# Attention's end in a hybrid decoder block: fillers that end 7 steps sooner, and the first out-projection row tile made piece by piece beside the last head's scores

## The chip, the cores and the metric

The kernel runs on one core of a Trainium2 chip. The metric is the device time of one execution in microseconds (us). The core's engines are TensorE (PE in the profile, with its weight loads as PEld), VectorE (DVE), ScalarE (ACT), GpSimd (POOL) and SyncE (SP), which here issues nearly all DMAs.

## The reference, cut to what matters

One block on 2048 tokens of width 1024, in float32: a norm with shift and scale from a condition vector, one input projection to q, k, v (512 each, 8 heads of 64) and u (512), stick-breaking attention on q, k, v, a pooling mixer on u, one output projection of both, a gated residual with a norm, and then the same frame around a SwiGLU feed-forward part.

```python
h = rmsnorm(x, g_mix_pre) * (1.0 + scale_m) + shift_m
q, k, v, u = jnp.split(h @ w_in, [SB_WIDTH, 2 * SB_WIDTH, 3 * SB_WIDTH], axis=-1)
# attention, strictly causal: for a query t and keys s < t
#   logw[t, s] = logsigmoid(z[t, s]) + sum over s < j < t of logsigmoid(-z[t, j])
attn = stick_breaking_attention(q, k, v)
pool = pooling_mixer(u, w_pool, pool_scale)
mix = jnp.concatenate([attn, pool], axis=-1) @ w_out
x = x + gate_m * rmsnorm(mix, g_mix_post)
h = rmsnorm(x, g_ffn_pre) * (1.0 + scale_f) + shift_f
f = (silu(h @ w_gate) * (h @ w_up)) @ w_down
x = x + gate_f * rmsnorm(f, g_ffn_post)
```

## The kernel before, in words

Matrix products are made from high and low parts. `split` (L56 to L59) casts a float32 tile to its high part on ACT and subtracts that on DVE to get the low part; `mm3` (L64 to L70) makes one product from three matmuls: high by high (L68), low by high (L69), high by low (L70). Three such matmuls of 128x128 by 128x512 are called a piece here.

The program has a prologue (norm, condition, first projections, v), attention from 322 us on, the output projection, and the feed-forward part from about 1040 us to the end.

Attention runs 320 steps: 8 heads, and in each head ten units of a query block of 512 and a key block of 512 or its left neighbours, in the order (0,0); (1,1), (1,0); (2,2), (2,1), (2,0); (3,3) to (3,0); four steps of 128 queries in each. A step of number n issues, in this order: the values product of a step turned three before (`values_step`, two matmuls, L875 and L876); the scores of step n (L827, L828), two sigmoids of them on ACT (L830, L832); one step later the scan that makes the running product on DVE (L843), and the product of both, the weights, on POOL (L849); then the turn of step n − 7 (`turn_step`): four PE transposes (L860) into a PSUM bank of the cycle `t_ps`, split into high (`wth`, ACT) and low (`wtl`, DVE) parts. Steps on the diagonal block are narrower for the scores (128 to 512 wide).

Into the steps go the fillers: the pieces of the remaining projections and small operations of the pooling mixer on POOL. How many pieces are due by a step is `goal`, which grows with the area of the steps so far and reaches its full count after END units of the 80; for END = 78 the last filler matmuls are at step 292, and the small operations end about ten steps behind. The output projection's weights are loaded when the fillers are through (two halves, `hb` and `ha`; one pair of loads in a step).

The output projection has 16 row tiles of 128 tokens, T0 to T15, in the order of SEQUENCE: 0, 4, 1, 5, 2, 6, 3, 7, 8 and so on. For one tile, `mix_load` (L931) loads the mixed rows (attention's and pooling's) and a low part, `mix_add` (L945) adds them on POOL, `mix_split` makes the two halves' high and low parts (`mh`, `ml`), and `mix_products` makes 16 pieces (two column halves by eight row blocks) into two PSUM banks from the cycle `f_ps`. `after_mix` (L1063 to L1084) squares both banks on ACT, makes the reciprocal root with a power on POOL (L113), scales on DVE (L1076), adds the residual on POOL (L1077), and makes the second norm in the same way: a square on ACT (L1080), a power on POOL, a scaling on DVE (L1083). `put_h2` (L1088) transposes the normed rows on PE (L122, `f_pt`) and writes the feed-forward's input.

T0 and T4 are the two first tiles. They are loaded, added and split inside the attention steps, at the step numbers in FIRST_LOADS, FIRST_ADDS and FIRST_SPLITS; their pieces are issued behind the last scores, three in each of the remaining steps (values and turns still come there), and the rest at the end. T1's rows go into memory of a pool (`op0`) that takes the place of attention's; the load waits for one of the last values matmuls.

Three things set the order of the work here. Until `order.close()` each engine gets its instructions in the order in which the code above issues them; behind it, a scheduler sets the order. Each engine runs its own instructions strictly in its order. [...]

Of the kernel before, what the change touches and what calls it, by code (L numbers as in the profile page):

```python
# [43 lines left out]
def block_kernel(ctx, tc, x, c, w_cond, b_cond, g_mix_pre, g_mix_post, w_in, w_pool,  # L44
# [98 lines left out]
    def psum(tag, bufs, name):  # L143
        return psp.tile([P, TB], F32, tag=tag, bufs=bufs, name=name)
# [7 lines left out]
    def bank_cycle(*tags):  # L152
        tags = itertools.cycle(tags)
        return lambda name: psum(next(tags), 1, name) if name else next(tags)

    z_ps, t_ps, av_ps, mm_only = bank_cycle("z0", "z1", "z2"), bank_cycle("w0", "w1"), bank_cycle("a0", "a1"), bank_cycle("mm")
# [661 lines left out]
    def weights_step(u, i):  # L818

        h, tb, sc = u  # L820
        diag = sc == tb
        kt, qt = kv[h, sc][0], qts[h, tb]
        L = (i + 1) * P if diag else TB
        nm = f"{h}_{tb}_{sc}_{i}"
        z = z_ps(f"z{nm}")
        keys = kt[:, 0:L]
        nc.tensor.matmul(z[:, 0:L], qt[:, 0, i * P:(i + 1) * P], keys, start=True, stop=False)  # L827
        nc.tensor.matmul(z[:, 0:L], qt[:, 1, i * P:(i + 1) * P], keys, start=False, stop=True)  # L828
        sg = att.tile([P, TB], F32, tag="sg", bufs=5, name=f"sg{nm}")
        nc.scalar.activation(sg[:, 0:L], z[:, 0:L], AF.Sigmoid, scale=0.125)  # L830
        pr = att.tile([P, TB + 1], F32, tag="pr", bufs=PRB, name=f"pr{nm}")
        nc.scalar.activation(pr[:, 0:L], z[:, 0:L], AF.Sigmoid, scale=-0.125)  # L832
        scans.append((u, i, pr, sg, L, nm))

    def scan_step(u, i, pr, sg, L, nm):

        diag = u[1] == u[2]
        carry = carries.pop(i, None)
        if carry is None:
            nc.gpsimd.memset(pr[:, L:L + 1], 0.0)  # L840
        else:
            nc.gpsimd.tensor_copy(pr[:, L:L + 1], carry)
        nc.vector.tensor_tensor_scan(pr[:, 0:L][:, ::-1], pr[:, 0:L][:, ::-1], begin[:, TB - L:][:, ::-1],  # L843
                                     zero if carry is None else carry, ALU.mult, ALU.max if diag else ALU.bypass)
        if u[2]:
            carries[i] = att.tile([P, 1], F32, tag=f"carry{i}", bufs=2, name=f"carry{nm}")
            nc.gpsimd.tensor_copy(carries[i], pr[:, 0:1])
        w = att.tile([P, TB], F32, tag="w", bufs=OFF + 4, name=f"w{nm}")
        nc.gpsimd.tensor_tensor(w[:, 0:L], sg[:, 0:L], pr[:, 1:L + 1], ALU.mult)  # L849
        wss.setdefault(u, []).append(w)  # L850

    def turn_step(u, b):

        h, tb, sc = u
        i0 = b if sc == tb else 0
        lo0 = i0 * P
        nm = f"{h}_{tb}_{sc}_{b}"
        wt = t_ps(f"wt{nm}")
        for i in range(i0, 4):
            nc.tensor.transpose(wt[:, i * P:(i + 1) * P], wss[u][i][:, b * P:(b + 1) * P], ident)  # L860
        wh = att.tile([P, TB], F32R, tag="wth", bufs=4, name=f"wth{nm}")
        wl = att.tile([P, TB], F32R, tag="wtl", bufs=4, name=f"wtl{nm}")
        split(wh[:, lo0:], wl[:, lo0:], wt[:, lo0:])
        return wh, wl, lo0

    def values_step(u, b, wh, wl, lo0):
        h, tb, sc = u
        hp, j = h // 2, h % 2
        first = sc == tb and b == 0
        last = sc == 0 and b == 3  # L870
        if first:
            avs[h, tb] = av_ps(f"av{h}_{tb}")
        av = avs[h, tb]
        vb = kv[h, sc][1][:, b, :]
        nc.tensor.matmul(av[:, lo0:], vb, wh[:, lo0:], start=first, stop=False)  # L875
        nc.tensor.matmul(av[:, lo0:], vb, wl[:, lo0:], start=False, stop=last)  # L876
        if last:
            end = (h, tb) == (HEADS - 1, NTB - 1)
            o1 = (up if end else wsp).tile([P, TB], F32, tag="um" if end else "o1", bufs=1, name=f"o1_{h}_{tb}")
            nc.scalar.copy(o1, av)  # L880
            for part, dst in enumerate((mtd, mld)):
                (nc.scalar if end else nc.sync).dma_start(dst[tb][hp, j * DH:(j + 1) * DH, :], o1[part * DH:(part + 1) * DH])

    def unit_loads(u):
        h, tb, sc = u
        if sc == tb:
            qts[h, tb] = block_loads(h, tb)
# [17 lines left out]
    area = [2.5 if tb == sc else 4.0 for _, tb, sc in units]  # L905
    wo, wo_next = [], 0
    HB_FREE = N_PIECES - 10 - 18 + 1
    END = 78
    START = 34
    for _ in range(START):  # L910
        next(fill)
# [5 lines left out]
    z_ps, t_ps, av_ps, mm_only = bank_cycle(*('z0', 'z1')), bank_cycle(*('w0', 'w1', 'a1')), bank_cycle(*('a0',)), bank_cycle(*('mm',))  # L917
    steps = [(u, i) for u in units for i in range(4)]

    def wo_load():  # L920
        nonlocal wo_next
        for l in range(2):
            nc.sync.dma_start(raw(wo[wo_next][l]), wod[wo_next][l])
        wo_next += 1
# [1 line left out]

    SEQUENCE = [sb * NT // 2 + half * 4 + i for sb in range(2) for i in range(4) for half in range(2)]
    mixed = {}
    f_ps = bank_cycle("z0", "z1", "z2", "mm", "w0", "w1", "a0", "a1")

    def mix_load(T):  # L931
        tb, cols = T // 4, slice((T % 4) * P, (T % 4 + 1) * P)
        m32 = (wst if T in SEQUENCE[:2] else op0).tile([P, KC, P], F32, tag="w32", name=f"m32_{T}")
        nc.sync.dma_start(m32, mtd[tb][:, :, cols].rearrange("k p t -> p k t"))
        if T in SEQUENCE[:2]:
            if not l32s:
                both = wst.tile([P, 2, TB], F32R, tag="e", bufs=1, name="l32s")
                l32s.extend(raw(both[:, n]).rearrange("p (k t) -> p k t", k=HK) for n in range(2))
            l32 = l32s.pop(0)
        else:  # L940
            l32 = wsp.tile([P, HK, P], F32, tag="o1", bufs=1, name=f"l32_{T}")
        nc.sync.dma_start(l32, mld[tb][:, :, cols].rearrange("k p t -> p k t"))
        return T, m32, l32

    def mix_add(T, m32, l32):  # L945
        nc.gpsimd.tensor_tensor(m32[:, 0:HK], m32[:, 0:HK], l32, ALU.add)
        return T, m32
# [17 lines left out]
                yield  # L965
        mixed[T] = pss

    FIRST_LOADS = (len(steps) - 14, len(steps) - 10)
    FIRST_SPLITS = (len(steps) - 3, len(steps) + 2)
    FIRST_ADDS = (len(steps) - 6, len(steps) - 1)  # L970
    PER_STEP = 3
    firsts, products, l32s = [], [], []

    def mix_pieces(count):
        while products and count:
            if next(products[0], 0) == 0:
                products.pop(0)
            else:
                count -= 1
# [3 lines left out]
    for n in range(len(steps) + OFF):  # L983
        begun = None
        if len(waiting) > LAG:
            begun = waiting.pop(0)
            if begun[1] or begun[0][1] != begun[0][2]:
                values_step(*begun)
                begun = None
        if n < len(steps):  # L990
            u, i = steps[n]
            if i == 0:
                unit_loads(u)
            weights_step(u, i)
            spent += 2.5 if u[1] == u[2] else 4.0
        if len(scans) > 1 or n >= len(steps) and scans:
            scan_step(*scans.pop(0))
        if n >= OFF:
            u, b = steps[n - OFF]
            waiting.append((u, b, *turn_step(u, b)))  # L1000
        if begun is not None:
            values_step(*begun)
        goal = START + (N_PIECES - START) * spent / (4 * sum(area[:END]))
        while fill is not None and taken < goal:
            taken += 1
            if next(fill, 0) == 0:
                fill = None
        for pool, here in ((hb, not wo and taken >= HB_FREE), (ha, len(wo) == 4 and fill is None)):
            if here:
                hi, lo = (pool.tile([P, 4, D], F32R, tag=tag, name=f"wo_{pool.name}{tag}")  # L1010
                          for tag in ("hi", "lo"))
                wo.extend((hi[:, k, :], lo[:, k, :]) for k in range(4))
        if wo_next < len(wo):
            wo_load()
        if n in FIRST_LOADS:
            firsts.append(mix_load(SEQUENCE[FIRST_LOADS.index(n)]))
        if n in FIRST_SPLITS:
            products.append(mix_products(*mix_split(*firsts.pop(0))))
        if n in FIRST_ADDS:
            firsts[0] = mix_add(*firsts[0])  # L1020
        if n >= len(steps):
            mix_pieces(PER_STEP)
    for a in waiting:
        values_step(*a)
        mix_pieces(PER_STEP)
# [90 lines left out]
    steps = []  # L1116
# [406 lines left out]
    steps, ops1_at = halves()  # L1523
# [91 lines left out]
```

## Time and profile before

| what | value |
|---|---|
| time, median of 3 runs | 2313.9 us (2313.23 to 2316.85) |
| the profiled execution's own time | 2318.17 us |
| its span | 2316.4 us (1.77 us lie outside it) |
| its mean granted PE clock | 0.993 of full speed |
| PE busy | 2261.0 us (98% of the span) |
| DVE busy | 1619.1 us (70%) |
| POOL busy | 1311.2 us (57%) |
| ACT busy | 1163.7 us (50%) |
| chain that ended last | PE 81%, DVE 7%, POOL 2%, DMA 2% |

The profile is of one execution, 4.3 us above the median of the runs. Busy times overlap, and a recorded matmul is longer than the time until the next one starts, so a PE that is 98% busy still has room. The view of stretches gives for each stretch its length, the busy time (and the number of instructions) of PE, PEld, DVE, ACT and POOL, then the granted PE clock, the DMA engines' share and GB/s. In timelines the columns are the start, the time it took, the engine, line, operation, output and inputs, the tile's shape, and how many alike follow one another; in brackets stands how long the engine was idle before, and what ended that.

### The profile page before, as it was taken

What the parts mean: (1) busy time and instruction counts of PE and PEld (TensorE: products, weight loads), DVE (VectorE), ACT (ScalarE), POOL (GpSimd) and SP (SyncE); (2) the same over time, 40 slices, a digit from 0 to 9 for tenths busy, and PEclk for the clock granted to TensorE, in tenths of its full rate; (3) what the DMA queues carried; (4) which work ended last, traced back from release to release, by engine and by line L of the source; (5) the groups of instructions that cost most, each with busy time, mean ns of one, the idle gap of its engine ahead of it and who ended that gap; (6) DMA issues with size and microseconds to landing.
All of it is one profiled execution on the core that took longest, in us unless ns stands there. A gap on an engine that the chain in (4) does not pass through costs nothing.

```text
span 2316.4 us, 33051 instructions
## 1 busy us (share of the span) xinstructions
PE 2261.0 (98%) x10605; PEld 1848.3 (80%) x10605; DVE 1619.1 (70%) x2215; ACT 1163.7 (50%) x2414; POOL 1311.2 (57%) x1616
## 2 busy tenths in 40 slices
PE   8999999999999999999999999999999999999997
PEld 4777878888888778887888888788888888888885
DVE  6764559999999966657656565887766556565556
ACT  4433659989998854444323222554433323234444
POOL 4452347787878845555787777331476565641004
PEclk9999999999999999999999999999999999999998
DMA  8885764433435535664545555876854333328554
GB/s 299 269 277 190 288 182 115 120 95 108 125 106 160 168 123 193 209 216 159 164 160 166 159 166 170 285 240 205 262 162 132 95 114 91 114 93 287 188 196 145
DMA packets 307114, 405.14 MB, mean 175 GB/s; under 512 B 19254, under 2 KB 179578, under 8 KB 303868
## 3 DMA queue, kind: packets, MB, share of 16 engines
q1 hardware_dynamic: 302620, 400.68, 54.0%
q10 hardware_dynamic: 4320, 2.36, 0.4%
q8 instruction: 83, 1.36, 0.2%
q14 instruction: 91, 0.75, 0.1%
HBM read 274.51 MB, written 128.45 MB: 174 GB/s over the span
## 4 chain that ended last, share of the span: by engine, by line
PE 81%; DVE 7%; POOL 2%; issue 2%; ACT 2%; DMA 2%; SPq 0%; POOLq 0%; DVEq 0%; ACTq 0%
PE wt L860 4%; PE t_u L70 3%; PE t_u L68 3%; PE t_u L69 3%; PE t_g L69 3%; PE t_g L68 3%; PE t_g L70 3%; DVE pr L843 3%; PE dn0p L69 3%; PE dn0p L70 3%; PE dn0p L68 3%; PE dn1p L69 3%; PE dn1p L68 3%; PE dn1p L70 3%; PE b_g L69 3%; PE b_u L69 3%
## 5 line engine op out<-in xcount | busy, mean ns | idle before, releaser
L849 POOL TENSOR_TENSOR w<-sg,pr 128x512 f32<-128x512 f32 (+2 forms) x320 | 307.3, 960 | 38.9 <-DVE pr L843 23.1
L1215 POOL TENSOR_TENSOR s<-s,cu 128x512 f32<-128x512 f32 x88 | 133.3, 1522 | 238.5 <-DVE cu L1214 137.8
L843 DVE TENSOR_TENSOR_SCAN pr<-pr,carry,begin 128x512 f32<-128x512 f32 x192 | 243.7, 1269 | 0.0
L830 ACT ACTIVATE sg<-z 128x512 f32<-128x512 f32 (+2 forms) x320 | 184.8, 578 | 45.1 <-PE z L828 33.4
L59 DVE TENSOR_TENSOR wtl<-wt,wth 128x512 fp32r<-128x512 f32 (+1 forms) x320 | 188.1, 588 | 17.5 <-ACT wth L58 16.7
L58 ACT CAST wth<-wt 128x512 fp32r<-128x512 f32 (+1 forms) x320 | 184.2, 576 | 13.4 <-PE wt L860 13.4
L832 ACT ACTIVATE pr<-z 128x512 f32<-128x512 f32 (+2 forms) x320 | 184.4, 576 | 0.0
L860 PE MATMUL wt<-ident,w 128*128 128x128 f32 x1088 | 173.7, 273 | 4.5 <-POOL pr L840 2.5
L59 DVE TENSOR_TENSOR u_s_l<-u_s,u_s_h 128x512 fp32r<-128x512 f32 x66 | 65.6, 995 | 151.9 <-ACT u_s_h L58 151.9
L860 PEld LDWEIGHTS wt<-ident,w 128*128 128x128 f32 x1088 | 134.2, 140 | 36.9 <-POOL pr L840 3.9
L1205 ACT ACTIVATE s<-s 128x512 f32<-128x512 f32 x88 | 55.7, 632 | 193.1 <-DVE s L1204 193.1
L875 PE MATMUL av<-wth,vt 128*128 128x512 f32 (+1 forms) x320 | 128.4, 401 | 0.8 <-ACT o L880 0.5
L69 PE MATMUL dn0p<-w0p_l,g0p_h 128*128 128x512 f32 x308 | 121.2, 394 | 1.3 <-DVE w0p_l L59 1.3
L876 PE MATMUL av<-wtl,vt 128*128 128x512 f32 (+1 forms) x320 | 119.1, 372 | 3.3 <-DVE wtl L59 2.9
L827 PE MATMUL z<-kt,qt 128*128 128x512 f32 (+2 forms) x320 | 118.3, 370 | 2.3 <-ACT pr L832 1.7
L68 PE MATMUL dn0p<-w0p_h,g0p_h 128*128 128x512 f32 x308 | 120.5, 391 | 0.0
L70 PE MATMUL dn0p<-w0p_h,g0p_l 128*128 128x512 f32 x308 | 120.4, 391 | 0.0
L59 DVE TENSOR_TENSOR u_a_l<-u,u_a_h 128x512 fp32r<-128x512 f32 x66 | 77.1, 1170 | 61.5 <-ACT u_a_h L58 61.5
L58 ACT CAST g_s_h<-g_s 128x512 fp32r<-128x512 f32 x66 | 39.5, 619 | 158.4 <-POOL g_s L1147 81.5
L828 PE MATMUL z<-kt,qt 128*128 128x512 f32 (+2 forms) x320 | 116.9, 365 | 0.0
L58 ACT CAST u_s_h<-u_s 128x512 fp32r<-128x512 f32 x66 | 38.6, 614 | 152.2 <-POOL u_s L1147 152.2
L69 PE MATMUL dn1p<-w1p_l,g1p_h 128*128 128x512 f32 x292 | 114.4, 392 | 0.0
(648 smaller groups left out, 7236.3 us busy)
## 6 DMA issues: line engine op xcount, KB each, us to landing
g<-in_w_gate_dram SPq DMA_DIRECT2D x42, 512.0 KB, 4.5
u<-in_w_up_dram SPq DMA_DIRECT2D x42, 512.0 KB, 5.2
wc<-in_w_cond_dram SPq DMA_DIRECT2D x32, 512.0 KB, 6.2
qt<-qd SPq DMA_DIRECT2D x64, 256.0 KB, 3.8
wd<-in_w_down_dram SPq DMA_DIRECT2D x44, 256.0 KB, 2.8
tdt<-wd SPq DMA_DIRECT2D x44, 256.0 KB, 2.0
w0p<-tdt SPq DMA_DIRECT2D x44, 256.0 KB, 3.1
w1p<-tdt SPq DMA_DIRECT2D x44, 256.0 KB, 2.8
```

The source lines that it names most:

```text
L58: nc.scalar.copy(hi, src)
L59: low.tensor_tensor(lo, src, raw(hi), ALU.subtract)
L68: nc.tensor.matmul(ps, lh, rh, start=first and i == 0, stop=False)
L69: nc.tensor.matmul(ps, lh, rl, start=False, stop=False)
L70: nc.tensor.matmul(ps, ll, rh, start=False, stop=last and i == n - 1)
L830: nc.scalar.activation(sg[:, 0:L], z[:, 0:L], AF.Sigmoid, scale=0.125)
L832: nc.scalar.activation(pr[:, 0:L], z[:, 0:L], AF.Sigmoid, scale=-0.125)
L843: nc.vector.tensor_tensor_scan(pr[:, 0:L][:, ::-1], pr[:, 0:L][:, ::-1], begin[:, TB - L:][:, ::-1], zero if carry is None else carry, ALU ...
L849: nc.gpsimd.tensor_tensor(w[:, 0:L], sg[:, 0:L], pr[:, 1:L + 1], ALU.mult)
L860: nc.tensor.transpose(wt[:, i * P:(i + 1) * P], wss[u][i][:, b * P:(b + 1) * P], ident)
L875: nc.tensor.matmul(av[:, lo0:], vb, wh[:, lo0:], start=first, stop=False)
L1215: nc.gpsimd.tensor_tensor(s, s, u, ALU.mult)
```

## The change

Five tables or constants change, all around attention's end.

- END goes from 78 to 76, so that the last filler matmuls are at step 285 instead of 292 and the small operations end about seven steps sooner too.
- T0 is loaded at step 299 instead of 306, added at 302 instead of 314, and split at 303 instead of 317. T4's step numbers (310, 319, 322) stay.
- From step 305 (FIRST_PIECES) on, one piece of T0 is issued in each step, so 15 of its 16 pieces stand in steps 305 to 319; from step 320 on there are three in each step, as before.
- At step 302 the turn's cycle of PSUM banks goes from three (w0, w1, a1) to two (w0, w1).
- The output projection's cycle of banks starts with mm and a1 instead of z0 and z1.

```diff
-    END = 78
+    END = 76
...
-    f_ps = bank_cycle("z0", "z1", "z2", "mm", "w0", "w1", "a0", "a1")
+    f_ps = bank_cycle("mm", "a1", "z0", "z1", "z2", "w0", "w1", "a0")
...
-    FIRST_LOADS = (len(steps) - 14, len(steps) - 10)
-    FIRST_SPLITS = (len(steps) - 3, len(steps) + 2)
-    FIRST_ADDS = (len(steps) - 6, len(steps) - 1)
+    FIRST_LOADS = (len(steps) - 21, len(steps) - 10)
+    FIRST_ADDS = (len(steps) - 18, len(steps) - 1)
+    FIRST_SPLITS = (len(steps) - 17, len(steps) + 2)
+    FIRST_PIECES = len(steps) - 15
...
-        if n >= len(steps):
-            mix_pieces(PER_STEP)
+        if n == FIRST_PIECES - 3:
+            t_ps = bank_cycle("w0", "w1")
+        if n >= FIRST_PIECES:
+            mix_pieces(PER_STEP if n >= len(steps) else 1)
```

T0 to T15 are the row tiles of the output projection by number, and step numbers are those of the loop over `n`. The added line count of three means that lines behind this place are 3 higher in the changed kernel.

On PE beside step 305 (wt is the output of a turn, av the values, z the scores, mix0 T0's product), before:

```order
L860 MATMUL wt7_2_1_2_10753<-ident_180,w7_2_1_2_10602 128x128
L860 MATMUL wt7_2_1_2_10753<-ident_180,w7_2_1_3_10628 128x128
L875 MATMUL av7_2_10681<-wth7_2_1_0_10704,vt7_1_10196 128x512
L876 MATMUL av7_2_10681<-wtl7_2_1_0_10705,vt7_1_10196 128x512
L827 MATMUL z7_3_3_2_10768<-kt7_3_10710,qt7_3_10712 128x384
```

and in the changed kernel:

```order
L860 MATMUL wt7_2_1_2_10774<-ident_180,w7_2_1_2_10612 128x128
L860 MATMUL wt7_2_1_2_10774<-ident_180,w7_2_1_3_10642 128x128
L68 MATMUL mix0_0_10783<-wo_hbhi_9592,mh_0_10723 128x512
L69 MATMUL mix0_0_10783<-wo_hblo_9593,mh_0_10723 128x512
L70 MATMUL mix0_0_10783<-wo_hbhi_9592,ml_0_10724 128x512
L875 MATMUL av7_2_10697<-wth7_2_1_0_10719,vt7_1_10215 128x512
L876 MATMUL av7_2_10697<-wtl7_2_1_0_10720,vt7_1_10215 128x512
L827 MATMUL z7_3_3_2_10789<-kt7_3_10731,qt7_3_10733 128x384
```

A piece of T0 has come between the transposes of a turn and the values.

On DVE beside step 322 (wtl are low halves of turned weights, ml_4 is the low part of T4's rows), before:

```order
L59 TENSOR_TENSOR wtl7_3_1_1_11128<-wt7_3_1_1_11122,wth7_3_1_1_11127 128x512
L59 TENSOR_TENSOR wtl7_3_1_2_11149<-wt7_3_1_2_11143,wth7_3_1_2_11148 128x512
L59 TENSOR_TENSOR wtl7_3_1_3_11169<-wt7_3_1_3_11163,wth7_3_1_3_11168 128x512
L59 TENSOR_TENSOR ml_4_11173<-m32_4_10896,mh_4_11172 128x512 x2
L59 TENSOR_TENSOR wtl7_3_0_0_11196<-wt7_3_0_0_11190,wth7_3_0_0_11195 128x512
```

and in the changed kernel, where mss0, mr0 and x1_0 are T0's first norm:

```order
L59 TENSOR_TENSOR wtl7_3_1_1_11175<-wt7_3_1_1_11169,wth7_3_1_1_11174 128x512
L1076 TENSOR_TENSOR mss0_11343<-mss0_11343 128x1
L111 TENSOR_SCALAR mr0_v_11348<-mss0_11343 128x1
L1079 SCALAR_TENSOR_TENSOR x1_0_11344<-mix0_0_10783,mr0_r_11350,gm_11339 128x512
L59 TENSOR_TENSOR wtl7_3_1_2_11189<-wt7_3_1_2_11183,wth7_3_1_2_11188 128x512
L59 TENSOR_TENSOR wtl7_3_1_3_11200<-wt7_3_1_3_11194,wth7_3_1_3_11199 128x512
L59 TENSOR_TENSOR ml_4_11204<-m32_4_10919,mh_4_11203 128x512 x2
```

The start of T0's norm has come ahead of the low halves of the turns 3_1_2 and 3_1_3, and of T4's low part.

On PE from T4's last piece to T1's first (f0 and f4 are transposes of the normed rows xr0 and xr4), before:

```order
L70 MATMUL mix4_1_11282<-wo_hahi_10762,ml_4_11173 128x512
L122 MATMUL f0_pt0_11448<-ident_180,xr0_11341 128x128 x4
L122 MATMUL f0_pt1_11461<-ident_180,xr0_11341 128x128 x4
L68 MATMUL mix1_0_11398<-wo_hbhi_9760,mh_1_11392 128x512
L69 MATMUL mix1_0_11398<-wo_hblo_9761,mh_1_11392 128x512
```

and in the changed kernel:

```order
L70 MATMUL mix4_1_11256<-wo_hahi_10595,ml_4_11204 128x512
L875 MATMUL av7_3_11027<-wth7_3_0_2_11267,vt7_0_10113 128x512
L876 MATMUL av7_3_11027<-wtl7_3_0_2_11268,vt7_0_10113 128x512
L875 MATMUL av7_3_11027<-wth7_3_0_3_11287,vt7_0_10113 128x512
L876 MATMUL av7_3_11027<-wtl7_3_0_3_11288,vt7_0_10113 128x512
L122 MATMUL f0_pt0_11448<-ident_180,xr0_11341 128x128 x4
L122 MATMUL f0_pt1_11461<-ident_180,xr0_11341 128x128 x4
L122 MATMUL f4_pt0_11558<-ident_180,xr4_11364 128x128
L68 MATMUL mix1_0_11398<-wo_hbhi_9592,mh_1_11392 128x512
```

T4's last piece has moved ahead of the two last values steps, and a transpose of T4's normed rows has come ahead of T1's first piece.

## The prediction

> **What bounds the kernel now.** All times are microseconds (us) unless a column says ns. I read the busy time of each engine in stretches first, then the timelines of PE, DVE, POOL, ACT and SP around attention's end. The stretches give the regime (columns: stretch, its length, busy PE, PEld, DVE, ACT, POOL, granted PE clock, DMA share, GB/s):
>
> ```profile
> span 2316.4 us, 33051 instructions
> 600.00:650.00 50.00, 49.95 (x287) 42.15 (x286) 50.00 (x65) 45.28 (x103) 38.20 (x85) 1.00 0.51 141
> 797.38:822.70 25.32, 21.92 (x117) 15.99 (x116) 23.97 (x30) 22.23 (x49) 22.00 (x48) 1.00 0.31 85
> 822.70:852.68 29.98, 29.98 (x145) 24.51 (x146) 14.46 (x23) 10.87 (x23) 12.08 (x13) 1.00 0.30 97
> 852.68:865.54 12.86, 12.34 (x57) 9.84 (x56) 8.46 (x16) 6.61 (x15) 5.71 (x5) 1.00 0.65 213
> ```
>
> In mid-attention DVE is busy throughout. 797.38 to 822.70 are steps 305 to 319, in which the change places its pieces: DVE still sets the pace there. From 822.70 to 852.68 PE is full: the 32 pieces of T0 and T4 (a piece is three matmuls), and the last values and turns. Behind that come T0's transposes and T1. So the change moves work from a stretch where PE is full into one where it isn't. What PE has to spare is read from starts, since a recorded matmul is longer than its place in the pipeline:
>
> ```profile
> 741.83 0.60 PE L860 MATMUL wt<-ident,w 128*128 128x128 f32 x4
> 742.19 0.48 PE L875 MATMUL av<-wth,vt 128*128 128x512 f32 x1
> 742.50 0.39 PE L876 MATMUL av<-wtl,vt 128*128 128x512 f32 x1
> 742.73 0.39 PE L827 MATMUL z<-kt,qt 128*128 128x512 f32 x1
> ...
> 823.61 0.48 PE L68 MATMUL mix<-wo_hbhi,mh 128*128 128x512 f32 x1
> 823.92 0.39 PE L69 MATMUL mix<-wo_hblo,mh 128*128 128x512 f32 x1
> 824.15 0.40 PE L70 MATMUL mix<-wo_hbhi,ml 128*128 128x512 f32 x1
> ```
>
> A transpose takes 0.36/4 = 0.09, a 512-wide matmul 0.23, and the first one behind transposes 0.31, so a changeover costs 0.08. The 117 matmuls of the 25.32 are 57 transposes (5.1), 48 of full width (11.0), 12 narrower ones (1.6, an estimate by width) and 15 changeovers (1.2): 18.9. PE can spare 25.3 − 18.9 = 6.4, while 15 pieces need 15 × 3 × 0.23 = 10.35. The stretch must grow even if nothing waits.
>
> **Steps up to 305.** The same filler work ends at step 285 instead of 292, so it is 7/285, 2 to 3%, denser. DVE, not PE, sets these steps, and its work is the same:
>
> ```profile
> 787.25 1.27 DVE L843 TENSOR_TENSOR_SCAN pr<-pr,carry,begin 128x512 f32<-128x512 f32 x1
> 789.02 1.27 DVE L843 TENSOR_TENSOR_SCAN pr<-pr,carry,begin 128x512 f32<-128x512 f32 x1
> 805.08 0.69 DVE L59 TENSOR_TENSOR wtl<-wt,wth 128x512 fp32r<-128x512 f32 x1 [1.27 <-ACT wth L58]
> ```
>
> A full step is 1.77 on DVE; a PE step without a piece is 1.37 (0.36 + 0.31 + 3 × 0.23), with one 2.06. More steps with a piece leave less room to catch up. I take +0.3, between −1.5 (a stall such as the 1.27 at 805.08, which small pool operations cause, gone with a little more) and +1.8 (one step of DVE).
>
> **Steps 305 to 319.** By PE's order beside step 305 (shown with the change) three matmuls now stand between a turn's transposes and the step's values and scores, and the scores feed ACT and then DVE. PE's work becomes 18.9 + 10.35 = 29.2 against DVE's 24.0: PE sets the pace. To this I add waits. T0's low halves are split at step 303, ahead of the weights' splits on DVE, and with two turn banks in place of three a turn waits for the split of the turn two before:
>
> ```profile
> 831.08 1.28 DVE L59 TENSOR_TENSOR ml<-m,mh 128x512 fp32r<-128x512 f32 x2
> ```
>
> That row shows 1.28 of DVE (both halves); it could hide wholly (0), or be paid with a like amount for the banks (2.6). I take 2.0, nearer the upper, since DVE has no idle time there to absorb it. Steps 305 to 319 then take 31.2 instead of 25.3: step 320 starts 5.9 later.
>
> The moves on the queues: T0's load passes the load of the last head's last queries on SP. That load is later by an issue or two; what hides it is the time until its first scores, and it costs as much as it lands beyond that. T0's add moves ahead on POOL to step 302, in room that the small pool operations leave. Both at nothing. The last output-weight loads move with the fillers' end, 7 × 1.77 = 12 sooner, and T0's products reach them from the fifth piece on. The changed bank cycle orders T0 into banks that are free early; nothing waits on it that I can find.
>
> **The tail.** 15 of T0's 16 pieces are gone from it: −10.35. But T0's norm now falls amid the last turns: in DVE's order at step 322, x1_0 stands ahead of the low halves of two turns and of ml_4, T4's operand. x1_0 needs a power from POOL, which stands behind POOL's last weight products; ml_4, and with it T4's first low product, waits behind that. The rows of T0's chain before show its lengths:
>
> ```profile
> 839.50 0.60 ACT L1072 ACTIVATE x<-mix 128x512 f32<-128x512 f32 x1
> 840.22 0.16 DVE L1073 TENSOR_TENSOR mss<-mss 128x1 f32<-128x1 f32 x1
> 841.23 1.41 DVE L1076 SCALAR_TENSOR_TENSOR x<-mix,mr_r,gm 128x512 f32<-128x512 f32 x2 [0.66 <-POOL mr_r L113]
> 842.12 2.54 POOL L1077 TENSOR_TENSOR x<-x,xr 128x512 f32<-128x512 f32 x2 [0.92 <-DVE x L1076]
> 844.70 1.06 ACT L1080 ACTIVATE xr<-x 128x1024 f32<-128x1024 f32 x1 [2.32 <-POOL x L1077]
> 846.70 0.75 DVE L1083 TENSOR_SCALAR xr<-x,fr_r 128x1024 f32<-128x1024 f32 x1 [0.66 <-POOL fr_r L113]
> ```
>
> From mss to x1_0's first half's end is 840.22 to 841.94, 1.7; a POOL product in front and the two splits and ml_4 behind (0.7 + 0.7 + 0.64) make some 3 to 4, of which PE covers under one piece. I take an idle of 2.8, between 0 and 4. T4's last matmul ends its place at 852.68 before; now −10.35 + 5.9 + 2.8 = −1.65, and less the two last values steps (4 × 0.23 = 0.92), which now come behind it, −2.6: 850.1.
>
> **T1's start.** This decides. In PE's order from T4 to T1, behind T4's last piece stand the two last values steps, T0's transposes and one transpose of T4's normed rows, f4_pt0, and only then T1. Two things now hold T1, each behind T4's last piece. First that transpose: it needs T4's whole norm, which T0's rows put at 839.50 to 847.45 = 7.95. Second T1's own load, whose memory is free when the values matmul L876 of weights 3_0_2 has read it:
>
> ```profile
> 846.45 0.40 PE L876 MATMUL av<-wtl,vt 128*128 128x512 f32 x1
> 852.45 0.39 PE L70 MATMUL mix<-wo_hahi,ml 128*128 128x512 f32 x1
> 852.68 1.03 PE L122 MATMUL f_pt<-ident,xr 128*128 128x128 f32 x8
> 854.13 0.50 PE L68 MATMUL mix<-wo_hbhi,mh 128*128 128x512 f32 x1 [0.41 <-ACT mh L58]
> 846.88 0.38 SPq L934 DMA_DIRECT2D m<-mtd  x1
> 850.85 1.29 POOL L946 TENSOR_TENSOR m<-m,l 128x512 f32<-128x512 f32 x1 [4.19 <-DMA m<-mtd]
> ```
>
> Before, that matmul ran 6 ahead of T4's end, and from it to T1's first matmul was 854.13 − 846.45 = 7.7, hidden under T4's pieces. Now it is behind T4's end: 850.1 + 0.2 + 7.7 = 858.0 by the load, 850.1 + 0.2 + 7.95 = 858.2 by the norm. T1 starts at 858.3, 4.2 later; its operands are then all there, which spares 0.3 of the short waits inside it before (855.44 follows 854.93 by 0.51): +3.9. PE, with 0.9 of values and 1.0 of transposes behind T4, is idle from 852.0 to 858.2, 6.2 in one piece. What an idle PE does to its clock:
>
> ```profile
> 1044.09 0.50 PE L68 MATMUL t_u<-t2h,u_s_h 128*128 128x512 f32 x1 [3.23 <-ACT u_s_h L58]
> 1044.00:1048.00 4.00, 3.50 (x9) 2.48 (x10) 3.52 (x5) 3.74 (x7) 0.63 (x1) 0.68 0.34 113
> 1048.00:1052.00 4.00, 4.00 (x18) 3.19 (x17) 3.06 (x5) 4.00 (x9) 0.00 (x0) 0.90 0.24 69
> 2293.81 0.79 PE L69 MATMUL dn1p<-w1p_10l,g1p_10h 128*128 128x512 f32 x1 [2.10 <-DVE w1p_10l L59]
> 2293.00:2297.00 4.00, 3.19 (x8) 2.51 (x9) 2.49 (x7) 1.44 (x3) 1.96 (x3) 0.50 0.21 80
> ```
>
> After 3.23 of idling the granted clock was 0.68 and 0.90: 4 × 0.32 + 4 × 0.10 = 1.7 lost. I charge that once, for the 6.2. At 2293 a wait of 2.10 among others went with a clock of 0.50, so the 2.8 at step 322 may cost as much again; I keep that for the upper end. The Trainium skill, "TensorE: Matmul & The Clock Gate", Part 1: The HAM clock gate, says that half rate comes after at least one idle window of about 3.4 us. By it the wait at step 322 costs no clock; the row at 2293 speaks against so sharp a limit.
>
> **Sum.** +0.3 (up to step 305) + 3.9 (T1's start) + 1.7 (clock) = +5.9. Behind T1 the same products run with PE full, so it stays. The profiled execution took 2318.17 (span 2316.4 and 1.77 around it) and would take 2324.1; the median of the runs is 4.3 below the profiled one, so I forecast 2313.9 + 5.9 = 2319.8. Measurement tells about 0.2% (4.6 us) from no change.
>
> **Rivals.** *Shorter wait or no clock loss* (32%): if ml_4 isn't late, T4 ends 2.8 earlier, T1 starts +1.1, and with the clock the sum is 0.3 + 1.1 + 1.7 = +3.1, 2317.0; if it is late and the clock holds, +4.2, 2318.1. For it: PE may do other turns while it waits; against: PE's order is fixed and ml_4 stands behind x1_0.
> *PE's spare time pays* (6%, faster): with no wait in steps 305 to 319 PE gains its 6.4 by T4's end, 846.3, and if T1's operands are there, T1 follows 1.9 behind it, at 848.2: −5.9, 2308.0. It decides for this if T1's load doesn't wait for the values step 3_0_2. Against it: that values step stands behind T4's last piece, so even with PE never idle T1 can't start before 846.3 − 0.9 + 0.2 + 7.7 = 853.3, 0.8 ahead of before, which the clock's 1.7 takes back. Only a gain ahead of step 305 could make it faster. The Trainium skill, "Perfetto Trace Analysis", Optimization Strategy, says that interleaving regimes with different bounds may improve performance; that is this rival, and the two stretches at the head are such regimes.
> *T4's norm goes slowly* (12%): in the rows of before T4's own norm took longer than T0's:
>
> ```profile
> 852.88 0.60 ACT L1072 ACTIVATE x<-mix 128x512 f32<-128x512 f32 x1 [1.01 <-PE mix L70]
> 861.66 1.77 DVE L1083 TENSOR_SCALAR xr<-x,fr_r 128x1024 f32<-128x1024 f32 x1 [0.66 <-POOL fr_r L113]
> ```
>
> That is 10.55, 2.6 over T0's, and T1 would be gated by it: +8.5, 2322.4; with a second clock loss +10.2, 2324.1. Against it: DVE's share of the difference was T0's transposed rows, now done earlier. *That the change doesn't do what it says* I leave without a chance, as the orders show the pieces moved.
>
> **Numbers.** Forecast 50%, the rivals 32, 12 and 6%. Slower by over 0.2%: 50 + 12 = 62%; within: 32%; faster: 6%. The range leaves out the faster case and goes from the bound with PE never idle (−0.8 − 0.3 + 1.7 = +0.6, less 1.0 of a gain ahead of 305, −0.4) to the slow norm with two clock losses (+10.2) with 0.9 more ahead of 305 (+11.1): 2313.5 to 2325.0.
>
> **What would show it.** Right: in the changed profile, step 320's transposes about 5.9 later and PE without long gaps from 797 on; a wait of T4's first low product for DVE of some 2.8; one PE gap of about 6 ahead of T1, ended by xr4, and a granted clock under 1 behind it. Wrong: T1 starting by 854, no such gap, a steady part behind T1 that is shorter, or steps ahead of 305 that took over 2 us less or more.

## The result, and the profile after

The changed kernel took 2336.2 us, median of 4 runs (2335.0 to 2336.69), against 2313.57 (2311.82 to 2316.85) for the kernel before: the ratio is 1.0095, with an interval of 1.0078 to 1.0113. It is slower by 22.6 us. The forecast was slower by 5.9, and the time lies beyond the range.

The profiled execution took 2335.88 us, with a span of 2334.0, so the spans differ by 17.6; the profiled execution of before was 4.3 above its median, which is nearly all of what is missing to 22.6. So a stretch that is shorter in the trace of after may only have been slow in that one execution of before.

The same landmarks in both traces split the 17.6. The first is the scan of step 0, the second that of step 300, the third T1's first matmul. Before:

```profile
318.99 1.11 DVE L843 TENSOR_TENSOR_SCAN pr<-pr,zero,begin 128x128 f32<-128x128 f32 x2
794.20 1.27 DVE L843 TENSOR_TENSOR_SCAN pr<-pr,carry,begin 128x512 f32<-128x512 f32 x1
```

and after (columns as in the prediction's timelines):

```profile
317.58 3.18 DVE L843 TENSOR_TENSOR_SCAN pr<-pr,zero,begin 128x128 f32<-128x128 f32 x4
805.62 1.27 DVE L843 TENSOR_TENSOR_SCAN pr<-pr,carry,begin 128x512 f32<-128x512 f32 x1
875.16 0.47 PE L122 MATMUL f_pt<-ident,xr 128*128 128x128 f32 x1 [5.65 <-DVE xr L1086]
875.29 0.77 PE L68 MATMUL mix<-wo_hbhi,mh 128*128 128x512 f32 x1
```

| stretch | before | after | difference |
|---|---|---|---|
| start to the scan of step 0 | 319.0 | 317.6 | −1.4 |
| scan of step 0 to scan of step 300 | 475.2 | 488.0 | +12.8 |
| scan of step 300 to T1's first matmul | 59.9 | 69.7 | +9.8 |
| T1's first matmul to the end | 1462.3 | 1458.7 | −3.6 |

The largest loss is where the prediction saw next to none: in the steps ahead of 300. In both kernels all filler matmuls and all attention work up to that scan are the same instructions, only woven together differently. Two sums of the pooling mixer on POOL come on top of that: before, the last two (some 2.5 us of POOL) come behind the scan of step 300, in steps 301 and 303; after, they come ahead of it.

The last row isn't the change's doing as it stands. The 12.8, the 9.8 and 1.7 more inside T1 make 24.3, while the medians differ by 22.6: that leaves some −1.7 for all the rest, an estimate from these numbers, and the part on the prediction shows that even this is within what one order of work varies by.

The end shows what the prediction described. PE waits for T4's operands, then idles ahead of T1. The stretches of after are steps 305 to 319 on PE, the tail to T4's last piece, the gap, and T1 (columns as in the prediction):

```profile
810.40:842.33 31.93, 29.89 (x157) 24.19 (x158) 28.12 (x33) 24.41 (x51) 20.43 (x46) 1.00 0.12 29
842.33:867.08 24.75, 21.60 (x94) 17.00 (x93) 10.40 (x18) 8.37 (x18) 7.15 (x8) 0.86 0.21 83
867.08:875.29 8.21, 2.32 (x14) 1.61 (x13) 4.08 (x11) 4.67 (x10) 4.80 (x5) 0.84 0.77 243
875.29:888.00 12.71, 12.71 (x48) 10.02 (x49) 5.81 (x8) 4.29 (x10) 1.29 (x1) 0.84 0.83 235
```

The first took 31.9 (forecast 31.2, before 25.3). The gap from T4's last matmul to T1's first is 8.2, as forecast, and the wait in it is ended by xr, T4's normed rows. In the tail the granted clock is 0.86, which the sum had left out.

### The profile page after: what moved, and what is told of

It reads as the page before. It is cut to its first block, busy times and chain, and to the rows that moved or that the text cites. A ratio compares the mean times of both kernels' runs of the same rounds, so it can differ in the third digit from the quotient of the medians.

```text
span 2334.0 us, 33065 instructions
## 1 busy us (share of the span) xinstructions
PE 2265.9 (97%) x10605; PEld 1854.0 (79%) x10605; DVE 1621.8 (69%) x2215; ACT 1165.4 (50%) x2414; POOL 1309.8 (56%) x1616
## 4 chain that ended last, share of the span: by engine, by line
PE 70%; DVE 10%; issue 5%; POOL 5%; ACT 3%; DMA 3%; SPq 0%; POOLq 0%; DVEq 0%; ACTq 0%
DVE pr L843 4%; PE wt L860 3%; PE dn0p L69 3%; PE dn0p L68 3%; PE dn0p L70 3%; PE dn1p L69 3%; PE dn1p L68 3%; PE dn1p L70 3%; PE t_u L69 3%; PE t_u L68 3%; PE t_u L70 3%; PE t_g L69 2%; PE t_g L68 2%; PE t_g L70 2%; PE mix L70 2%
## 5 line engine op out<-in xcount | busy, mean ns | idle before, releaser
L849 POOL TENSOR_TENSOR w<-sg,pr 128x512 f32<-128x512 f32 (+2 forms) x320 | 306.1, 956 | 45.4 <-DVE pr L843 24.3
L59 DVE TENSOR_TENSOR u_s_l<-u_s,u_s_h 128x512 fp32r<-128x512 f32 x66 | 65.5, 992 | 151.9 <-ACT u_s_h L58 151.9
```

Source lines behind the costliest of these rows:

```text
L59: low.tensor_tensor(lo, src, raw(hi), ALU.subtract)
```

## What the steps ahead of 300 wait for

The view of waits, from the first scan to that of step 300, says which engine held up which. Before (columns: engine and group, what it waited for, us in total, times, longest):

```profile
ACT sg L830 <- PE z L828: 31.0, 74, 0.9
DVE wtl L59 <- ACT wth L58: 9.3, 24, 0.8
PEld wt L860 <- POOL pr L840: 2.7, 5, 1.4
PE wt L860 <- POOL pr L840: 1.5, 3, 1.2
```

and after:

```profile
ACT sg L830 <- PE z L828: 37.1, 86, 1.1
DVE wtl L59 <- ACT wth L58: 19.7, 35, 1.8
PEld wt L860 <- POOL pr L840: 8.2, 7, 2.1
PE wt L860 <- POOL pr L840: 6.5, 7, 1.9
```

DVE, which sets the pace, is busy for nearly as long in both (465.3 and 467.0), but waits 10.4 us more for the casts of turns, its only wait that grows; the turn's transposes on PE wait 5.0 more for POOL, and the sigmoids 6.1 more for scores. One such place in after, on PE and on POOL:

```profile
461.42 0.49 PE L860 MATMUL wt<-ident,w 128*128 128x128 f32 x3
463.22 0.33 PE L860 MATMUL wt<-ident,w 128*128 128x128 f32 x1 [1.31 <-POOL pr L840]
```

```profile
459.53 1.09 POOL L849 TENSOR_TENSOR w<-sg,pr 128x512 f32<-128x512 f32 x1
460.58 1.29 POOL L381 TENSOR_TENSOR um<-us,um 128x512 f32<-128x512 f32 x1
461.81 0.18 POOL L842 COPY pr<-carry 128x1 f32<-128x1 f32 x1
462.08 1.09 POOL L849 TENSOR_TENSOR w<-sg,pr 128x512 f32<-128x512 f32 x1
463.11 0.10 POOL L840 MEMSET pr<- 128x1 f32 x1
```

A sum of the pooling mixer (L381, a filler's small operation) stands between two weight products. The second product ends at 463.17, and the turn's fourth transpose, which reads it, starts 1.3 late. Turn, cast, split and values of that step are late by as much, and DVE with them:

```profile
464.21 0.69 DVE L59 TENSOR_TENSOR wtl<-wt,wth 128x512 fp32r<-128x512 f32 x1 [1.13 <-ACT wth L58]
```

A POOL step is 1.09 + 0.18 + 0.18 of the 1.77 that DVE takes, so a sum of 1.29 doesn't fit into one.

## Experiments

Theory 1 (density): denser fillers make the steps ahead of 300 slower, more the denser they are. Theory 2 (alignment): it counts where a piece or a small sum falls. Theory 3 (the end): the loss belongs to T0's early add, split and pieces. "Steps 0 to 300" is the time from scan to scan in that kernel's trace, worked out as above. Each kernel was timed together with runs of the kernel before, whose median was 2314.0 to 2315.2 in these sets; "+" is the distance from the median beside it, and behind the time stand the ratio to it and the ratio's interval.

### One part at a time

END alone, on the kernel before:

```diff
-    END = 78
+    END = 76
```

> The kernel before with END = 76 alone. Theory (density): the 7 steps' worth of filler pieces that are pushed into the steps ahead of 285 cost there what the profile of the changed kernel shows up to the scan of step 300, some 12.8 us behind that of step 0; nothing is given back at the end, so 2323 to 2327 us. Rival (the end): the loss belongs to T0's earlier split and pieces; then the end of the fillers alone costs 0 to 3 us, 2313 to 2317 us.

It took 2326.47 (1.0048, 1.0033 to 1.0063): +12.5. Steps 0 to 300 took 488.1, as in the changed kernel. More than half of the loss is this one number.

The rest alone, with END put back to 78 in the changed kernel:

```diff
-    END = 76
+    END = 78
```

> The changed kernel with END back at 78: T0 earlier and its pieces beside the scores, fillers as before. Theory (density): the steps up to 300 are as before, and what is left is the end's part, from the scan of step 300 to T1's start some 7 us, less some 3.5 given back behind T1: 2317 to 2321 us. It may be a few us more, because the output weights are loaded later and small pool operations stand beside T0's add. Rival (the end): nearly the whole loss stays, 2330 us or more.

It took 2326.29 (1.005, 1.0035 to 1.0065): +12.3, several us above what theory 1 left for the end. Steps 0 to 300 took 474.8, as before; but at step 303 it lost 6.2 where the changed kernel loses 3.0, with PE waiting for T0's cast:

```profile
800.74 0.80 PE L68 MATMUL mix<-wo_hbhi,mh 128*128 128x512 f32 x1 [3.70 <-ACT mh L58]
```

So with END at 78 T0's early steps cost more, since the fillers' last sums still run beside them: on POOL a sum starts at 797.55, T0's add directly behind it at 798.77, and ACT, which stands 5.3 before T0's cast, goes on at 800.07. The two parts, 12.5 and 12.3, make 24.8 against 22.6 together. Theory 3 as the whole cause falls; it holds for half.

END = 77 in the changed kernel:

```diff
-    END = 76
+    END = 77
```

> The changed kernel with END = 77, halfway. Theory (density): the loss up to step 300 is about half of 12.8 us, so 2328 to 2331 us. Rival (alignment): what counts is where a small pool operation or a piece falls beside a unit's narrow steps, not how dense they are; then the time can lie anywhere, also outside the two ends with 76 and 78.

It took 2330.93 (1.0067, 1.005 to 1.0084), inside theory 1's range; steps 0 to 300 took 480.0, +4.8. This fits density and doesn't exclude alignment.

The changed kernel with T0's pieces put back:

```diff
-    FIRST_PIECES = len(steps) - 15
+    FIRST_PIECES = len(steps)
```

> The changed kernel with T0's pieces (and the two turn banks) put back behind the last scores; fillers, loads, add and split stay early. Theory (density): +12.8 us up to step 300 and some 3 us for T0's split at step 303 stay, and T1 starts without a gap: 2326 to 2330 us. Rival (the end): the pieces were the loss, and the time is 2314 to 2319 us.

It took 2330.6 (1.0068, 1.0053 to 1.0083), +16.6, just above theory 1's range. Steps 0 to 300 took 488.1, step 303 lost 3.0, and between T4 and T1 PE waited 0.4, as before. With the first run this makes a ladder: END +12.5, the early load, add and split 4.1 more, the pieces beside the scores with the two turn banks 6.0 more.

### POOL's part of the fillers

The pooling sums left out, with END = 78 and 76:

```diff
+            if tb > 1:
+                yield lambda: None
+                step *= 2
+                continue
...
-                nc.gpsimd.tensor_tensor(m, prev[:, 16:], m, ALU.subtract)
```

> The kernel before (END = 78) with the pooling mixer's sums on POOL for the second half of the tokens left out (16 + 7 additions of about 1.1 and 1.3 us, among the fillers), so its output isn't the reference's. It is the base for the next kernel. Steps 0 to 300, from scan to scan, took 475.2 us with the sums. If the sums never delay a step, 475; if POOL's place in the chain matters, less: 470 to 474 us.

> The same (sums left out) with END = 76. Theory (POOL): denser fillers cost because small sums on POOL fall beside weight products that PE's turns wait for; without the sums END = 76 costs 0 to 4 us of the 12.8 over steps 0 to 300. Rival (PE): the pieces on PE themselves cost it; then it still costs 9 to 13 us.

They took 2309.43 (0.9976, 0.9967 to 0.9985) and 2316.49 (1.0009, 1.0 to 1.0019). (The trace of before has 28 such sums, 20 and 8, not 16 + 7; these kernels have none.) Steps 0 to 300 took 472.6 and 477.7: without the sums END = 76 costs 5.1 there, not 12.8. Neither theory as put: 7.7 of the loss goes with the sums on POOL, and 5.1 stays.

To see whether that rest is POOL too, the low halves of the fillers' weights, which POOL makes, were left out as well (the products then take the high half twice; of the fillers only twelve copies of 0.2 us are left on POOL):

```diff
-        split(c[1][:, ks, :], c[2][:, ks, :], c[0][:, ks, :], nc.gpsimd)
+        if attending:
+            nc.scalar.copy(c[1][:, ks, :], c[0][:, ks, :])
+        else:
+            split(c[1][:, ks, :], c[2][:, ks, :], c[0][:, ks, :], nc.gpsimd)
```

> END = 78 with neither the small sums nor the low halves of the fillers' weights made on POOL (the high half is used in their place), so its output isn't the reference's: no filler work on POOL at all. Base for the next kernel: steps 0 to 300 in 466 to 472.6 us.

> The same with END = 76. Theory (all POOL): without filler work on POOL the denser fillers cost 0 to 2 us over steps 0 to 300. Rival (PE's pieces or late loads): the 5.1 us that were left without the sums stay, 4 to 6 us, in single waits of PE for loads or of ACT for PE.

They took 2309.3 (0.9978, 0.9966 to 0.9989) and 2314.62 (0.9998, 0.9987 to 1.0008); steps 0 to 300 took 472.1 and 477.6. The 5.5 is still there, so it isn't filler work on POOL. The waits from 318 to 800 us, a little past step 300 in both, with 78 and then with 76:

```profile
ACT sg L836 <- PE z L834: 26.5, 63, 0.9
DVE wtl L59 <- ACT wth L58: 7.0, 20, 0.6
```

```profile
ACT sg L836 <- PE z L834: 31.7, 82, 0.9
DVE wtl L59 <- ACT wth L58: 11.0, 25, 1.1
```

ACT waits 5.2 more for scores, 82 times instead of 63 (up to step 300 alone it is 6.6 more), and DVE 4.0 more for casts. That points to the pieces on PE, ahead of the scores; no run took the pieces alone away, so this part is argued and not shown. The fillers' own casts on ACT and splits on DVE come denser too, and no run excludes them.

### Density or alignment

END = 80 on the kernel before, so that fillers are thinner:

```diff
-    END = 78
+    END = 80
```

> The kernel before with END = 80 alone: fillers spread over two units more. Theory (density, all the way): thinner fillers gain over steps 0 to 300 as denser ones lost, 3 to 8 us there, but the fillers and the output weights now end later and may hold up T0: 2308 to 2318 us. Rival (alignment): 78 happens to miss the collisions on POOL, and 80 meets others: steps 0 to 300 take 3 us or more longer, 2317 to 2326 us.

It took 2329.23 (1.0066, 1.0053 to 1.008): +14.5, a larger loss than with 76. Up to step 180 it was 0.2 ahead; then one wait took most:

```profile
615.56 0.44 PE L827 MATMUL z<-kt,qt 128*128 128x128 f32 x1 [8.48 <-DMA kt<-kd]
```

The keys of that unit, which the fillers make, weren't there in time. Neither theory had that: spread too thin, the fillers miss their due time. Steps 0 to 300 took 489.1.

One piece fewer, and two more, ahead of step 0, with END = 78:

```diff
-    START = 34
+    START = 33
```

> The kernel before with 33 pieces instead of 34 ahead of the first step: fillers 0.5% denser, all pieces shifted. Density: steps 0 to 300 take 0 to 3 us longer, in small parts. Alignment: 4 us or more longer, in a few places, as END = 77 with its 4.8 at 1.3% denser.

> The kernel before with 36 pieces ahead of the first step: fillers 1% thinner, 1.4 us more ahead of attention. Density: steps 0 to 300 take 0 to 5 us less. Alignment: they take 3 us or more longer all the same, because 34 and 78 together are where the pieces miss POOL's full steps.

With 33 the time was 2316.7 (1.0008, 0.9999 to 1.0018), with 36 it was 2320.81 (1.0025, 1.0015 to 1.0034). Steps 0 to 300 took 480.7 (+5.5, at 0.5% denser) and 479.9 (+4.6, at 1% thinner). With 33 the whole time isn't clear of noise: in its trace the scan of step 0 comes 3.8 sooner than in that of before, and the part behind T1 is 3.3 shorter; both vary between executions (see below), while steps 0 to 300 repeat within 0.7 us.

Every other placing that was tried (END 76, 77 and 80, START 33 and 36) costs 4.6 us or more in these steps, denser or thinner; with 80, 8.5 of the 13.9 are the late keys. Theory 1 as the whole cause falls: 1% thinner fillers should have gained, and they lost 4.6. Theory 2 fits: 34 and 78 together are a placing with few collisions, and every shift that was tried leaves it. That density adds to it for END = 76, which loses more than twice as much as the smaller shifts, isn't excluded.

### The end

T0's add two steps sooner in the changed kernel:

```diff
-    FIRST_ADDS = (len(steps) - 18, len(steps) - 1)
+    FIRST_ADDS = (len(steps) - 20, len(steps) - 1)
```

> The changed kernel with T0's add two steps sooner (300 instead of 302), all else as changed. Theory: at step 303 ACT stands with its sigmoids behind T0's cast, which waits for an add that POOL comes to only then; with the add sooner the stall of 3.0 us at step 303 shrinks to 1 or less: 2333 to 2335 us. Rival: the stall is the split's own 1.76 us on DVE and T0's late load; then it stays, 2336 us.

It took 2332.72 (1.0081, 1.0064 to 1.0098): +17.5, where the changed kernel was +22.6 (the bare medians differ by 3.5). Step 303 lost 1.3 instead of 3.0, a little more than the 1 or less of the theory; DVE's split of T0 takes 1.34 there. So of the 3.0 the wait for the add is 1.7, and the rest is the split. In the changed kernel ACT's row shows the stall, which the profile puts down to a DMA; POOL's row shows that the add ended at 810.88, as the cast began:

```profile
810.91 1.14 ACT L58 CAST mh<-m 128x512 fp32r<-128x512 f32 x2 [2.31 <-DMA m<-mtd]
```

```profile
809.61 1.27 POOL L946 TENSOR_TENSOR m<-m,l32s 128x512 f32<-128x512 f32 x1
```

The add stands in POOL's order behind the weight products of steps that POOL does late, and ACT's sigmoids of the next steps stand behind the cast.

One piece per step in the tail of the changed kernel:

```diff
-    PER_STEP = 3
+    PER_STEP = 1
```

> The changed kernel with one piece in each step behind the last scores too (PER_STEP = 1), so that the last values steps come ahead of T4's last pieces, and no transpose of T4 stands ahead of T1. Theory: T1's gap (5.7 us) and the half clock behind it (about 1.7) go, and the wait for T4's operand with its half clock shrinks: 6 to 11 us less, 2325 to 2330 us. Rival: the tail's steps are bound by the chain from POOL over the turn to the values, and PE only idles elsewhere: 2333 us or more.

It took 2327.01 (1.0051, 1.0036 to 1.0066): +11.8, so 9.2 less than the changed kernel by the bare medians and 10.8 by the distances from before. T1 followed T4 without a wait, as the last values steps now come ahead of T4's last pieces. The part on T4's operand was wrong: that wait stayed (1.19 and 1.83, as in the changed kernel). The traces show 8.6 of the gain, the gap ahead of T1 and the clock behind it: 7.3 from the scan of step 300 to T1's first matmul, and 1.3 from there to T5's, the next tile's.

### A better version

With END at 78, the add at 300 and one piece per tail step, then with T0 behind POOL's last sums and half of its pieces beside the scores, and one or two per tail step:

```diff
-    FIRST_LOADS = (len(steps) - 21, len(steps) - 10)
-    FIRST_ADDS = (len(steps) - 18, len(steps) - 1)
-    FIRST_SPLITS = (len(steps) - 17, len(steps) + 2)
-    FIRST_PIECES = len(steps) - 15
-    PER_STEP = 3
+    FIRST_LOADS = (len(steps) - 17, len(steps) - 10)
+    FIRST_ADDS = (len(steps) - 13, len(steps) - 1)
+    FIRST_SPLITS = (len(steps) - 10, len(steps) + 2)
+    FIRST_PIECES = len(steps) - 8
+    PER_STEP = 1
```

> T0 earlier and beside the scores with END at 78, the add at step 300 and one piece in each tail step: what the three runs on single parts showed, put together. Theory (the parts add): 2326.3 less 3.5 (the add) less 9.2 (the tail) is 2313 to 2316 us. Rival (a stall is only moved): with END at 78 POOL's small sums still run at step 300, and the stall at step 303 stays: 2318 us or more.

> END at 78; T0 added at step 307, behind POOL's last small sums, split at 310, its pieces from 312 on (8 of 16 beside the scores), then one piece in each tail step. Theory: ACT no longer waits for the add, and DVE isn't kept from T4's operand by T0's norm, since T0 ends in the tail; PE saves what it could spare in 8 steps, 2 to 4 us: 2309 to 2313 us. Rival (PE's spare time isn't usable): the pieces delay scans as much as they spare the tail: 2313 to 2318 us.

> The same with two pieces in each tail step. Theory: PE is fuller in the tail than with one, and three pieces and T0's transposes still cover part of T1's load: 2308 to 2313 us. Rival (T1's load): the last values steps run only three pieces ahead of T4's end, so T1 waits some 4 us for its load, and the clock with it: 2314 to 2319 us.

(The diff is that of the second kernel against the changed one with END at 78.) The first took 2314.17 (0.9999, 0.999 to 1.0008), inside its range: the parts' gains add up and come out even with before; some 2.4 at step 303 stay. The second took 2309.3 (0.998, 0.9971 to 0.9988), the third 2312.16 (0.9987, 0.9978 to 0.9996). Both beat the kernel before, whose runs beside them had a median of 2314.69; the second is 5.4 faster. Both are inside their ranges. In the second's trace T1 comes 57.8 behind the scan of step 300 (59.9 before); for the rest of its gain see below.

## Why the prediction was wrong, step by step

**Steps up to 305: +0.3 forecast, +12.8 measured by step 300.** This is the step that failed, and it alone is more than the rest of the miss. It argued that DVE sets these steps and that its work stays the same. The work did stay the same (465.3 us busy before, 467.0 after), but DVE isn't free of the others: its split waits for a cast, the cast for a turn on PE, the turn for POOL, and all four have little room in a step. The prediction had the number for PE: a step with a piece takes 2.06 there, more than the 1.77 of DVE, so where pieces fall matters; it put that at +0.3. The bound of +1.8, one step of DVE, had no reason in the rows; the row at 805.08, quoted there as a stall that could go, was an example of what would come more often. With END = 76 alone that one stall did go (step 306 took 1.50 instead of 2.88), as the lower bound had it, while the steps ahead lost 12.8. That no neighbouring placing of the fillers is as good couldn't be read from one trace, but that the stalls in it were few for so full a pipeline could.

**Steps 305 to 319: 31.2 forecast, 31.9 measured.** The count of matmuls by their starts was right, and PE does set the pace there. Of the waits, 2.0 in the sum, the split was as assumed: step 303 loses 1.3 to it even with the add sooner. (The prediction said that DVE has no idle time there; its own row has 1.35, 23.97 busy of 25.32.) That ACT would stand behind T0's cast for an add on POOL wasn't seen. At step 303, ahead of these steps, split and add together cost 3.0, with END at 78 even 6.2.

**The wait for T4's operands: 2.8 forecast, 3.0 measured,** in two parts around two matmuls:

```profile
846.96 0.50 PE L68 MATMUL mix<-wo_hbhi,mh 128*128 128x512 f32 x1 [1.19 <-ACT mh L58]
847.30 0.39 PE L69 MATMUL mix<-wo_hblo,mh 128*128 128x512 f32 x1
849.51 0.80 PE L70 MATMUL mix<-wo_hbhi,ml 128*128 128x512 f32 x1 [1.82 <-DVE ml L59]
850.11 0.63 PE L68 MATMUL mix<-wo_hbhi,mh 128*128 128x512 f32 x1
850.53 0.63 PE L69 MATMUL mix<-wo_hblo,mh 128*128 128x512 f32 x1
...
855.23 0.53 PE L70 MATMUL mix<-wo_hbhi,ml 128*128 128x512 f32 x1
855.60 0.39 PE L68 MATMUL mix<-wo_hahi,mh 128*128 128x512 f32 x1
```

The mechanism of the second is the forecast one: on DVE x1_0 waits 1.46 for POOL's power, and two low halves and ml stand behind it. With T0's pieces put back and in the faster version, where no T0 norm stands there, PE has no such wait. The wait for the cast mh wasn't forecast. And matmuls then start 0.43 apart instead of 0.23 until 855.6, with a granted clock of 0.50 from 849 to 855: some 2.6 lost. The sum had kept that for the upper end. The Trainium skill, "TensorE: Matmul & The Clock Gate", Part 1: The HAM clock gate, gives an idle window of about 3.4 us as the condition for half rate; here the longest wait is 1.82 and both together 3.0, so by that rule no loss was due. The measurement decides, and the row at 2293 in the prediction had pointed the same way.

**T1's start: right in mechanism and size.** T1 comes 8.2 behind T4's end, as forecast; its gap is ended by T4's normed rows. With one piece per tail step the gap goes, which shows that the order is its cause. The clock behind it: from T1's first matmul to T5's it takes 13.1 instead of 11.4, 1.7 more, as forecast; that the size fits is in part luck, since its price came from a wait of 3.23 and the wait here is 5.65.

**Behind T1: forecast unchanged, measured 3.6 less from T1 on, although T1 itself loses 1.7.** The prediction said that the same products run with PE full. Before, PE waits in the out-projection for DVE:

```profile
PE mix L68 <- DVE x L1076: 3.6, 3, 1.7
```

In the changed kernel and in the faster version that view lists no waits of PE there. But this isn't shown to be a gain of the change. Nine other kernels run PE in before's order from T1 on, and there the same wait is 1.1 to 2.8 in total (2.4 with END = 76 alone); in the three others that run it in after's order it is 0.7, 2.3 and 1.3. From T5's first matmul to the last tile's last piece it is 156.3 before and 153.6 to 155.6 in those nine, 151.9 after and 152.7 to 154.7 in those three. So the trace of before is the longest of ten, that of after the shortest of four, and the means are 154.8 and 153.3, 1.5 apart, with ranges that overlap. The faster version has 152.0; of its 5.4 us, 2.1 lie ahead of T1, and where the rest lies isn't shown.

So from the scan of step 300 to T1's first matmul the forecast was +4.2, and the traces have +9.8. The 5.6 of difference are 1.6 ahead of step 305, from the stall at step 303, 0.7 in steps 305 to 319, and 3.3 in the tail, of which 2.6 are the clock. The gap ahead of T1 was right. The 12.8 ahead of step 300 weren't in any rival. The range was too narrow because the bounds for 300 steps were taken from single stalls.

What stays open: whether the last 5.5 us of the steps ahead of 300 come from the pieces on PE or from the fillers' work on ACT and DVE, and why END = 76 loses more than twice as much as the smaller shifts.

## What to carry to other kernels

Where four engines are near full in a loop, a number that spreads filler work over it sets a phase, not just a density: price it by trying its neighbours, and don't put a term at nothing because the work is the same. Before moving an operation ahead by hand, ask for each engine in order what it will wait for and what stands behind it: here one cast behind a late add held up the sigmoids of the next steps. And moving work off a full tail helps only if enough of it stays to cover what the next stage waits for: here PE stood 5.65 us for T4's norm, ahead of T1.

## What wasn't expected of the hardware

Two PE waits of 1.19 and 1.82 us with two matmuls between them went with a granted clock of 0.50 from 849 to 855 us in the changed kernel; one piece per tail step left the waits in place, and the clock was 0.50 there again. Attention's steps repeat closely where the order is the same: steps 0 to 300 took 488.0, 488.1, 488.1, 487.8 and 488.1 in five kernels with END = 76, and 475.2, 474.8, 474.8, 475.3 and 474.6 in five with 78. The out-projection doesn't: from T5 to its last piece ten kernels with the same order on PE took 153.6 to 156.3.
